# Low parts of the projections' weights made by ScalarE and an accumulating transfer in place of VectorE

## The chip, the core and the metric

The kernel runs on one core of one Trainium2 chip. Its time is the device time of one execution in microseconds (us); the median of several runs is what counts. One further execution was taken with the hardware profiler: its page and its trace are the source of every row below.

## What is computed

One inference step of a decoder layer, for 512 prompt tokens and 8 sampling tokens together (T = 520 columns). Cut to what matters here:

```python
hn = rms_norm(x, p['norm_mix'][l])
z = jnp.einsum('bld,de->ble', hn, p['w_in'][l])             # 2048 -> 4096
xa, ga, xb, gb, zc = jnp.split(z, [...], axis=-1)
# three token mixers side by side: RG-LRU (xa, ga), convolution (xb, gb), chunked gating (zc)
mix = jnp.concatenate([y_a, y_b, y_c], axis=-1)
x = x + jnp.einsum('blm,md->bld', mix, p['w_out'][l])       # 2048 -> 2048
hf = rms_norm(x, p['norm_ffn'][l])
ff = jnp.square(jax.nn.relu(jnp.einsum('bld,df->blf', hf, p['w_ff1'][l])))
x = x + jnp.einsum('blf,fd->bld', ff, p['w_ff2'][l])
y = rms_norm(x, p['norm_final'])
```

All of it is float32. A matrix product is made of three products of a shorter type, `fp32r`: each operand is split into a high part (the value rounded to fp32r) and a low part (the value less its high part, rounded likewise), and high x high, high x low and low x high are added up in PSUM.

## The kernel before

The two projections are cut into **units**. A unit is 1024 rows by 128 columns of a weight matrix, stored as a tile of 128 partitions x 1024 elements (512 KB), and holds eight 128x128 blocks. There are 96: units 0 to 63 are the input projection `w_in`, units 64 to 95 the output projection `w_out`. Then follow the two large products of the MLP, whose items are made by other code (`split_item`, `product`; lines 1071 to 1170) that the change does not touch.

Each unit passes through these steps. SyncE loads it into one of seven `raw` tiles (`load`, L149). ScalarE copies it, rounded, into a `whi` tile (`hi_part`, L154). VectorE writes raw less high into a `wlo` tile (`lo_part`, L160); after that the raw tile may be loaded again. TensorE then does 48 matmuls of 260 columns (`matmuls`): for each of the eight blocks two with high weights and high activations (L177), two with high weights and low activations (L179), two with low weights and high activations (L181). `whi` and `wlo` have four buffers each. A unit's high part can therefore be written once the matmuls of the unit four before it are done.

The order on every engine is written out by hand: an instruction runs in the order in which the program issues it on its engine, and waits there for what it needs. The main loop runs over units and MLP items, `i = 0` to `NU - 1`, and issues in this order: loads that may go (`more_weights`: up to five units ahead, and while more than one raw tile is free), the high part of unit `i + 3` (`AHEAD` is 3), the low part of unit `i + 3`, the matmuls of unit `i`, and, where a group of units is complete, its reading out of PSUM (`evac1`, L723 to L747). Last, `run(credit)` issues pieces of the mixers' work (L485 to L690: convolution, norms, gates, recurrence), by a budget of constants for each unit. Units 0 to 3 are split and multiplied in pieces as the activations arrive; units 4 to 7 are split ahead of the loop (low parts up to 7 are done there).

GpSimd does nothing large until the MLP. In the projections it only clears the heads of the padded tiles `xaf` and `ubf` (memsets, L700 and L713); from about 610 us it issues stores and loads of MLP operands (L905, L913, L1094). SyncE's queue also holds small loads and stores of the mixers (L489, L613, L690, L758), and issues in order, so loads of weights often go out several at a time behind one of these.

Of the kernel before, what the change touches and what calls it, by code (L numbers as in the profile page):

```python
# [6 lines left out]
F32R = mybir.dt.float32r  # L7
AF = mybir.ActivationFunctionType
ALU = mybir.AluOpType
# [57 lines left out]
def trunk_kernel(tc, xT, vecs, w_in, w_out, w_ff1, w2, ca_st, h0_st, cb_st, gate_w, sgu_wT, sgu_b,  # L67
                 yT, ca_o, lh_o, cb_o, cv_o):
    nc = tc.nc
    V, S, P, PE = nc.vector, nc.scalar, nc.gpsimd, nc.tensor  # L70
    from contextlib import ExitStack
    with ExitStack() as es:
# [5 lines left out]
        wp = es.enter_context(tc.tile_pool(name="wp", bufs=1))  # L78
# [8 lines left out]
        def nm(s):  # L87
            cnt[0] += 1
            return f"{s}_{cnt[0]}"
# [36 lines left out]
        raws, whis, wlos = {}, {}, {}  # L126
# [6 lines left out]
        def raw_drop(r):  # L133
            rfree.append(r[1])
# [16 lines left out]
        def hi_part(i, a=0, b=8):  # L151
            if i not in whis:
                whis[i] = wp.tile([128, 1024], F32R, tag="whi", name=nm("whi"), bufs=4)
            S.activation(out=whis[i][:, a * 128:b * 128], in_=raws[i][0][:, a * 128:b * 128], func=AF.Copy)  # L154

        def lo_part(i, a=0, b=8):
            if i not in wlos:
                wlos[i] = wp.tile([128, 1024], F32R, tag="wlo", name=nm("wlo"), bufs=4)
            sl = slice(a * 128, b * 128)
            V.tensor_tensor(out=wlos[i][:, sl], in0=raws[i][0][:, sl], in1=whis[i][:, sl].bitcast(F32),  # L160
                            op=ALU.subtract)
            if b == 8:
                raw_drop(raws.pop(i))
# [94 lines left out]
        def require(flag, name):  # L258

            if flag in flags:  # L260
                return
            while flag not in flags:
                if isinstance(advance(name), Wait):
                    for n in queues:
                        if n != name and queues[n]:
                            advance(n)
# [43 lines left out]
        units = []  # L310
# [15 lines left out]
        NP = len(units)  # L326
        LD, AHEAD = 4, 3
# [150 lines left out]
        sig, ubf, xaf, graw = {}, {}, {}, {}  # L478
# [214 lines left out]
        def evac1(kind, c, ps, mode=0):  # L693

            if kind == "xa":
                if mode < 2:
                    if c >= 2:
                        require(("conv_a", c - 2), "a")
                    xaf[c] = Tt(c % 2, 552)
                    P.memset(xaf[c][:, 0:3], 0.0)  # L700
                o = xaf[c][:, 3:3 + T].rearrange("p (h n) -> p h n", h=2)
            elif kind == "ga":
                if mode < 2:
                    mixt[c] = Mt(c)
                o = hv(mixt[c])
            elif kind == "gb":
                if mode < 2:
                    sig[c] = Zt()
                o = hv(sig[c])
            elif kind == "xb":  # L710
                if mode < 2:
                    ubf[c] = Tt(12 + c, 552)
                    P.memset(ubf[c][:, 0:30], 0.0)  # L713
                o = ubf[c][:, 30:30 + T].rearrange("p (h n) -> p h n", h=2)
            elif kind == "vc":
                mixt[12 + c] = Mt(12 + c)
                o = hv(mixt[12 + c])
            else:
                require(("head", 7), "a")
                gu[c] = Tt(5 + c)  # L720
                o = hv(gu[c])
            if mode == 1:
                S.activation(out=o, in_=pv(ps), func=AF.Copy)  # L723
                return
            V.tensor_tensor(out=o, in0=o if mode else pv(ps), in1=hv(R), op=ALU.mult)
            if kind == "xa":
                push("a", g_head(c))
                if c > 0:
                    require(("gates", c - 1), "a")
                    load_gate(c)  # L730
            elif kind == "ga":
                S.activation(out=mixt[c], in_=mixt[c], func=AF.Gelu_apprx_tanh)
            elif kind == "gb":
                S.activation(out=sig[c], in_=sig[c], func=AF.Sigmoid)
            elif kind == "xb":
                u = ubf[c][:, 30:30 + T]
                V.tensor_tensor(out=u, in0=u, in1=sig.pop(c), op=ALU.mult)
                push(f"b{c % 2}", g_conv_b(c))
                if c == 3:
                    push("n", g_norm_b())  # L740
            elif kind == "vc":
                S.activation(out=mixt[12 + c], in_=mixt[12 + c], func=AF.Gelu_apprx_tanh)
                if c == 3:
                    push("c", g_norm_c())
                    push("c", g_sgu())
            else:
                S.activation(out=gu[c], in_=gu[c], func=AF.Gelu_apprx_tanh)  # L747
                flags.add(("uc", c))
# [327 lines left out]
        for q in quads[32:]:  # L1076
            i, a, b = WIN[q.win]
# [153 lines left out]
        lo_done = 7  # L1231
        credit = 0.0
        for i in range(NU):
            it[0] = i
            if i > 3:
                more_weights()
            if 7 < i + AHEAD < NP:
                hi_part(i + AHEAD)
            while lo_done < min(i + AHEAD, NP - 1):
                lo_done += 1  # L1240
                lo_part(lo_done)
            run_due("v", i)
            if NP <= i + AHEAD < NU:
                split_item(i + AHEAD - NP)
            run_due("a", i)
            if i < NP:
                u = units[i]
                kind = u.grp[0]
                if i > 3:
                    matmuls(i, u)  # L1250
                if i == NP - 1:
                    for c in range(8, 16):
                        free.extend([(ap_, f"Ah{c}"), (ap_, f"Al{c}")])
            else:
                if i == NP:
                    psp.release()
                    ps2.append(es.enter_context(tc.tile_pool(name="ps2", bufs=1, space=bass.MemoryType.PSUM,
                                                             reuse_waits="tile")))
                product(i - NP)
                more_operands()  # L1260
                if i - NP == H1_DONE + 2:
                    fin = last_norm(1)
                if i - NP >= H1_DONE + 2:
                    next(fin, None)
            if i >= NP:
                continue
            if u.stop:
                ps = ps_of.pop(u.grp)
                if kind == "out":
                    kh, m = u.grp[1:]  # L1270
                    V.tensor_tensor(out=hv(x1[m]), in0=pv(ps), in1=hv(x1[m]), op=ALU.add)
                    if kh:
                        hf_half(m % 8, m // 8)
                elif i <= 6:
                    held.append(u.grp)
                    evac1(u.grp[0], u.grp[1], ps, 1)
                else:
                    evac1(kind, u.grp[1], ps)
            if i == 6:
                ps = bsum(ssum[0])  # L1280
                rstd(pv(ps), hv(R), hv(Zt()), 1.0 / D)
                V.tensor_scalar(Rp, R, 1.0, None, op0=ALU.min)
                for g in held:
                    evac1(g[0], g[1], None, 2)
            if i == 62:

                for c in range(8):
                    require(("y_a", c), "a")
                    mx[c] = At(c)
                    split_to(mx[c], mixt[c])  # L1290
                load_x1(0)
                load_x1(1)
            if i == 63:
                flags.add("hn")
            if kind == "out":
                kh, m = u.grp[1:]
                if kh == 0 and m + 2 < 16:
                    load_x1(m + 2)
                if kh == 0 and m == 15:
                    for c in range(8, 16):  # L1300
                        require(("mx", c), "c" if c >= 12 else "n")
                    drain()
                    mc.release()
                    xp = es.enter_context(tc.tile_pool(name="xp", bufs=1, reuse_waits="tile"))
                    free += [(mp, f"M{c}") for c in range(8, 16)] + [(tp, f"T{c}") for c in range(8, 16)]
                    free += [(xp, f"E{c}") for c in range(NX)]
                    for c in range(8):
                        free += [(ap_, f"Ah{c}"), (ap_, f"Al{c}")]
            if i < 80:
                credit = min(credit + UNIT_US - 1.2 - (1.0 if u.stop else 0.0), 6.0)  # L1310
                credit -= run(credit)
            else:
                run(0.7)
# [90 lines left out]
```

## Time and profile before

| | |
|---|---|
| median of 3 runs | 1910.35 us (1909.89 to 1910.84) |
| the profiled execution | 1910.32 us |
| its span (first to last instruction) | 1908.6 us |
| TensorE's mean granted clock | 0.994 |
| TensorE busy | 1874.4 us (98%) |
| VectorE busy | 1563.5 us (82%) |
| ScalarE busy | 968.5 us (51%) |
| GpSimd busy | 264.0 us (14%) |
| projections, matmuls of units 4 to 95 | 32.6 to 583.8 us |

The page gives the busy time of each engine and its share of the span; PE is TensorE (PEld its loads of weights), DVE VectorE, ACT ScalarE, POOL GpSimd, SP SyncE. In timelines the first two numbers are the start and the length in us, then come engine, line, operation and tiles (output<-inputs) and how many instructions one line merges. A bracket at the end gives the time that the engine stood idle before, and what ended it. "To landing" is the time from a transfer's issue to its arrival. Lines are those of the kernel before.

### The profile page before, as it was taken

The numbers are of one execution on the slowest core, as the hardware profiler recorded it, in microseconds if no ns is written. First come the engines' busy times: TensorE is split into PE (matmuls) and PEld (weight loads), VectorE is DVE, ScalarE is ACT, GpSimd is POOL, SyncE is SP. The second block draws the span as 40 slices with busy tenths as digits, with TensorE's granted clock in tenths as the row PEclk, the third lists the DMA queues.
The fourth block names the chain that finished last, engine by engine and source line by source line (L and its number), as shares of the span: only waits on it lengthen the run. The fifth ranks groups of instructions, "written<-read, shape, count | busy, mean of one in ns | idle before, by whom it ended". The sixth has DMA issues, their size and how long they took to land.

```text
span 1908.6 us, 38079 instructions
## 1 busy us (share of the span) xinstructions
PE 1874.4 (98%) x15540; PEld 1869.0 (98%) x15540; DVE 1563.5 (82%) x2206; ACT 968.5 (51%) x1443; POOL 264.0 (14%) x499
## 2 busy tenths in 40 slices
PE   8999999999999999999999999989999999999995
PEld 8999999999999999999999999989999999999994
DVE  7878777565688889899888888877798888888888
ACT  7445345562235666666666666644444444444453
POOL 0000000000000122122111121530312112112000
PEclk9999999999999999999999999999999999999997
DMA  6223223133343656656555555883757657647324
GB/s 253 106 95 117 72 95 114 59 139 113 122 167 124 217 200 218 216 201 220 202 184 209 194 197 206 302 319 103 277 162 241 228 197 236 204 153 262 116 85 134
DMA packets 113072, 336.82 MB, mean 176 GB/s; under 512 B 16768, under 2 KB 25600, under 8 KB 112896
## 3 DMA queue, kind: packets, MB, share of 16 engines
q1 hardware_dynamic: 73200, 205.35, 32.1%
q0 software_dynamic: 38400, 127.83, 18.9%
q8 instruction: 122, 2.00, 0.4%
q10 hardware_dynamic: 1296, 1.19, 0.2%
q14 instruction: 54, 0.44, 0.1%
HBM read 265.44 MB, written 68.87 MB: 175 GB/s over the span
## 4 chain that ended last, share of the span: by engine, by line
PE 95%; DVE 2%; DMA 1%; issue 1%; POOL 1%; ACT 0%; SPq 0%; DVEq 0%; POOLq 0%; ACTq 0%
PE psA L1167 12%; PE psA L1170 12%; PE psA L1169 12%; PE ps L181 10%; PE ps L179 10%; PE ps L177 10%; PE psD L1169 6%; PE psD L1167 6%; PE psD L1170 6%; PE psB L1170 3%; PE psB L1167 3%; PE psB L1169 3%; DVE X L1223 1%; DVE wlo L1147 0%; DMA raw<-w 0%
## 5 line engine op out<-in xcount | busy, mean ns | idle before, releaser
L1145 ACT ACTIVATE whi<-raw 128x1024 fp32r<-128x1024 f32 (+5 forms) x532 | 488.9, 921 | 327.5 <-PE psD L1169 143.1
L1147 DVE TENSOR_TENSOR wlo<-raw,whi 128x1024 fp32r<-128x1024 f32 (+5 forms) x532 | 558.8, 1051 | 88.2 <-ACT whi L1145 86.7
L1170 PE MATMUL psA<-o,wlo 128*128 128x260 f32 x2048 | 578.4, 282 | 2.8 <-DVE wlo L1147 2.8
L1167 PE MATMUL psA<-o,whi 128*128 128x260 f32 x2048 | 578.5, 282 | 1.9 <-DVE X L974 0.7
L1169 PE MATMUL psA<-o,whi 128*128 128x260 f32 x2048 | 577.8, 282 | 0.0
L1167 PEld LDWEIGHTS psA<-o,whi 128*128 128x128 f32 x2048 | 385.3, 188 | 3.2 <-DVE X L974 1.2
L1170 PEld LDWEIGHTS psA<-o,wlo 128*128 128x128 f32 x2048 | 385.2, 188 | 3.2 <-DVE wlo L1147 3.2
L1169 PEld LDWEIGHTS psA<-o,whi 128*128 128x128 f32 x2048 | 385.2, 188 | 0.0
L1101 DVE TENSOR_TENSOR raw<-raw,raw 128x1024 f32<-128x1024 f32 (+6 forms) x304 | 318.8, 1049 | 29.3 <-DMA raw<-w 28.9
L177 PE MATMUL ps<-Ah,whi 128*128 128x260 f32 x1536 | 311.5, 284 | 5.8 <-ACT Ah L356 5.8
L179 PE MATMUL ps<-Al,whi 128*128 128x260 f32 x1536 | 310.7, 284 | 0.0
L181 PE MATMUL ps<-Ah,wlo 128*128 128x260 f32 x1536 | 310.2, 283 | 0.0
L1170 PE MATMUL psD<-o,wlo 128*128 128x260 f32 x1024 | 289.3, 282 | 1.2 <-DVE wlo L1147 1.2
L1167 PE MATMUL psD<-o,whi 128*128 128x260 f32 x1024 | 289.8, 283 | 0.0
L1169 PE MATMUL psD<-o,whi 128*128 128x260 f32 x1024 | 289.7, 283 | 0.0
L177 PEld LDWEIGHTS ps<-Ah,whi 128*128 128x128 f32 x1536 | 238.4, 189 | 6.3 <-ACT Ah L356 6.1
L181 PEld LDWEIGHTS ps<-Ah,wlo 128*128 128x128 f32 x1536 | 238.2, 189 | 0.0
L179 PEld LDWEIGHTS ps<-Al,whi 128*128 128x128 f32 x1536 | 237.4, 190 | 0.6 <-DVE Al L359 0.6
L905 POOL DMA_DIRECT2D fx<-o x224 | 121.6, 543 | 815.3 <-DVE o L794 569.3
L1170 PEld LDWEIGHTS psD<-o,wlo 128*128 128x128 f32 x1024 | 192.8, 188 | 1.4 <-DVE wlo L1147 1.4
L1169 PEld LDWEIGHTS psD<-o,whi 128*128 128x128 f32 x1024 | 193.0, 188 | 0.0
L1167 PEld LDWEIGHTS psD<-o,whi 128*128 128x128 f32 x1024 | 192.7, 188 | 0.0
(207 smaller groups left out, 2282.7 us busy)
## 6 DMA issues: line engine op xcount, KB each, us to landing
raw<-w_ff SPq DMA_DIRECT2D x128, 512.0 KB, 4.1
fx<-o POOLq DMA_DIRECT2D x224, 260.0 KB, 3.1
o<-fx POOLq DMA_DIRECT2D x224, 260.0 KB, 5.0
raw<-w SPq DMA_DIRECT2D x116, 384.0 KB, 3.7
raw<-w_in SPq DMA_DIRECT2D x62, 512.0 KB, 6.0
raw<-w_out SPq DMA_DIRECT2D x32, 512.0 KB, 5.6
raw<-w SPq DMA_DIRECT2D x32, 448.0 KB, 3.5
z<-x1d POOLq DMA_DIRECT2D x32, 260.0 KB, 3.2
```

Of the source, the lines that this page charges most:

```text
L177: PE.matmul(ps[:, h, :H], hi[:, kk], xh[:, h * H:(h + 1) * H], start=st, stop=False)
L179: PE.matmul(ps[:, h, :H], hi[:, kk], xl[:, h * H:(h + 1) * H], start=False, stop=False)
L181: PE.matmul(ps[:, h, :H], lo[:, kk], xh[:, h * H:(h + 1) * H], start=False, stop=sp)
L905: P.dma_start(fxd[i][2 * g - 1 + n if g else 0], t[0][:, :].bitcast(F32))
L1101: V.tensor_tensor(out=o[0][:, :n], in0=x[0][:, :n], in1=y[0][:, :n], op=ALU.add)
L1145: S.activation(out=whis[i][:, :n], in_=r[0][:, :n], func=AF.Copy)
L1147: V.tensor_tensor(out=wlos[i][:, :n], in0=r[0][:, :n], in1=whis[i][:, :n].bitcast(F32), op=ALU.subtract)
L1167: PE.matmul(ps, hi[:, kk], xh, start=first and j == 0, stop=False, skip_group_check=True)
L1169: PE.matmul(ps, hi[:, kk], xl, start=False, stop=False, skip_group_check=True)
L1170: PE.matmul(ps, lo[:, kk], xh, start=False, stop=j == q.q - 1 and p in (("P2", "P3", "Q4", "P7") if q.late else ("P2", "P3", "Q4")), skip_ ...
L1223: V.scalar_tensor_tensor(out=x, in0=x, scalar=vc(V_FIN + m), in1=o, op0=ALU.mult, op1=ALU.mult)
```

## The change

For units 8 to 95 the low part is no longer made by VectorE. A new function, `both_parts`, takes the place of `hi_part` in the loop: ScalarE writes the high part as before, then a second time with scale -1, so that the low tile holds the negative of the high part. The raw tile is given up at once. GpSimd then issues a transfer that reads the unit's weights from memory once more, adds them to what stands in the low tile, and converts to fp32r: weights less high part, as before. Units 0 to 7 keep `lo_part`. The memsets of the padded tiles go from GpSimd to VectorE.

```diff
+        def both_parts(i):
+
+            hi_part(i)
+            wlos[i] = wp.tile([128, 1024], F32R, tag="wlo", name=nm("wlo"), bufs=4)
+            S.activation(out=wlos[i], in_=raws[i][0], func=AF.Copy, scale=-1.0)
+            raw_drop(raws.pop(i))
+            P.dma_start(wlos[i], units[i].src, accum_op=ALU.add)
...
-                    P.memset(xaf[c][:, 0:3], 0.0)
+                    V.memset(xaf[c][:, 0:3], 0.0)
...
-                    P.memset(ubf[c][:, 0:30], 0.0)
+                    V.memset(ubf[c][:, 0:30], 0.0)
...
             if 7 < i + AHEAD < NP:
-                hi_part(i + AHEAD)
-            while lo_done < min(i + AHEAD, NP - 1):
+                both_parts(i + AHEAD)
+            while lo_done < min(i + AHEAD, 7):
                 lo_done += 1
                 lo_part(lo_done)
```

## Rows read from the trace of the kernel before

**Rows 1.** The page: busy us (share of span) xinstructions, and the last chain's engines.

```profile
PE 1874.4 (98%) x15540; PEld 1869.0 (98%) x15540; DVE 1563.5 (82%) x2206; ACT 968.5 (51%) x1443; POOL 264.0 (14%) x499
...
PE 95%; DVE 2%; DMA 1%; issue 1%; POOL 1%; ACT 0%; SPq 0%; DVEq 0%; POOLq 0%; ACTq 0%
```

**Rows 2.** Windows: stretch, its us, busy of each engine; clock, DMA share, GB/s.

```profile
core 0: us, PE busy (x) PEld busy (x) DVE busy (x) ACT busy (x) POOL busy (x), PEclk, DMA share, GB/s
...
50.00:583.00 533.00, 533.00 (x4433) 532.40 (x4431) 388.16 (x575) 234.32 (x317) 0.72 (x8) 1.00 0.31 108
```

**Rows 3.** TensorE's waits: total us, times, longest; up to 700 us, then all.

```profile
PE ps L177 <- ACT Ah L356: 5.8, 2, 5.6
...
PE side L1202 <- DVE fsum L955: 6.7, 1, 6.7
...
PE psA L1170 <- DVE wlo L1147: 2.8, 2, 1.8
```

**Rows 4.** Lines L160 and L154: ns min/median/max, first and last start.

```profile
L160 DVE TENSOR_TENSOR wlo<-raw,whi x108: 415/1218/1228, 4.9 to 565.2; 128x1024 fp32r<-128x1024 f32 x92, 128x256 fp32r<-128x256 f32 x16
...
L154 ACT ACTIVATE whi<-raw x108: 398/1045/1065, 4.5 to 564.0; 128x1024 fp32r<-128x1024 f32 x92, 128x256 fp32r<-128x256 f32 x16
```

**Rows 5.** Line L1094, GpSimd's plain reads of 260 KB: issue ns, and landing us.

```profile
L1094 POOL DMA_DIRECT2D o<-fx x224: 546/546/563, 1196.5 to 1763.5; - x112
...
DMA to landing us min/median/max: 2.8/5.0/8.8
```

**Rows 6.** DMA view: issues of 316:328 and 60:63; the load queue of 389:406.

```profile
raw<-w_in SPq DMA_DIRECT2D x3, 512.0 KB, 3.6
...
raw<-w_in SPq DMA_DIRECT2D x5, 512.0 KB, 5.9
...
q1 hardware_dynamic: 1961, 5.36, 88.7%
```

**Rows 7.** Timeline of ScalarE, late in the projections: unit 93's high part.

```profile
552.46 1.04 ACT L154 ACTIVATE whi<-raw 128x1024 fp32r<-128x1024 f32 x1
```

**Rows 8.** Timeline of TensorE: first matmuls of units 10, 11, 61, 66, 93.

```profile
68.04 0.40 PE L177 MATMUL ps<-Ah,whi 128*128 128x260 f32 x2
...
68.52 0.28 PE L181 MATMUL ps<-Ah,wlo 128*128 128x260 f32 x1
...
73.80 0.40 PE L177 MATMUL ps<-Ah,whi 128*128 128x260 f32 x2
...
375.64 0.59 PE L177 MATMUL ps<-Ah,whi 128*128 128x260 f32 x2
...
404.62 0.41 PE L177 MATMUL ps<-Ah,whi 128*128 128x260 f32 x2
...
566.32 0.40 PE L177 MATMUL ps<-Ah,whi 128*128 128x260 f32 x2
```

**Rows 9.** Timeline of ScalarE: high parts of units 10, 11 and 12, 61 and 62, 66.

```profile
59.83 1.04 ACT L154 ACTIVATE whi<-raw 128x1024 fp32r<-128x1024 f32 x1
...
68.05 1.99 ACT L154 ACTIVATE whi<-raw 128x1024 fp32r<-128x1024 f32 x2
...
369.54 1.99 ACT L154 ACTIVATE whi<-raw 128x1024 fp32r<-128x1024 f32 x2
...
396.55 1.04 ACT L154 ACTIVATE whi<-raw 128x1024 fp32r<-128x1024 f32 x1
```

**Rows 10.** Timeline of VectorE: the subtraction of unit 10 and what follows.

```profile
65.65 1.22 DVE L160 TENSOR_TENSOR wlo<-raw,whi 128x1024 fp32r<-128x1024 f32 x1
66.78 0.69 DVE L725 TENSOR_TENSOR M<-ps,R 128x520 f32<-128x520 f32 x1
```

**Rows 11.** Timeline of SyncE's queue: two of the bursts of loads.

```profile
60.39 2.31 SPq L149 DMA_DIRECT2D raw<-w_in  x5
...
366.93 1.98 SPq L149 DMA_DIRECT2D raw<-w_out  x4
```

## The prediction

> **What bounds the kernel now.** I read the page first: its busy shares put TensorE at 98% of the span, VectorE at 82%, ScalarE at 51%, and in the chain of work that ended last 95% is TensorE and 2% VectorE [rows 1]. An average says little of one stage, so the table of windows came next, for the stretch that the change touches: units 8 to 95 of the projections. From 50 to 583 us TensorE is busy for all 533.00 us, at a granted clock of 1.00, while VectorE has 388 of them and the DMA engines 31% [rows 2]. Then the list of waits: in the first 700 us TensorE waited 5.8 us in all, twice, for the first activations (L356), before unit 8 is reached; its other waits (seven more lines of the list, the longest two 6.7 and 2.8 us) are in the second half or at the end, for L955, L1147 and their like, which the change leaves alone [rows 3]. So where VectorE is relieved, nobody waits for VectorE, and the stage lasts as long as its matmuls. What can still move the time is the other side: a low part that comes too late for its matmuls.
>
> **What goes.** 88 of the 108 subtractions L160 leave VectorE, those of units 8 to 95, 1.218 us each at the median [rows 4]: 88 x 1.218 = 107 us of VectorE's time. Worth on the path: 0, since TensorE waits for none of it [rows 2, 3]; VectorE's list of work after each unit is budgeted by constants in the code, and does not grow. Twelve small memsets come to VectorE from GpSimd, at some 0.1 us each, and are hidden in VectorE's idle 145 us of that stretch [rows 2].
>
> **What comes: ScalarE.** 88 activations that write the negative high part into the low tile. The nearest row is L154, the same tile and shape, at 1.045 us [rows 4]: 92 us, for an engine with some 234 of 533 us in use [rows 2]. Each stands directly behind L154 of its unit, so the low part starts its second leg about 1.04 us after the high part is done. Queued behind it on ScalarE are the gelu, sigmoid and square operations, which have the earlier VectorE in their favour: where ScalarE waits for VectorE, it now waits 1.2 us less per subtraction that stood in front.
>
> **What comes: GpSimd and the transfer.** 88 transfers of 512 KB, which read the weights in memory again and add them to the low tile. GpSimd has nothing else to do until its stores near 610 us. An issue costs it 0.546 us at the median [rows 5]. From the issue to the landing there is no row of an accumulating transfer, so I bound it. Lower end: a plain load of the same 512 KB on idle queues, 3.6 us [rows 6]. An accumulating one also has to read what stands in the tile. In the crowded stretch from 389 to 406 us the engines moved 5.36 MB at 88.7% busy, so 512 KB are 17 x 0.887 / 5.36 x 0.524 = 1.47 us of all 16 engines [rows 6]: one pass. With one more pass the transfer lands after 3.6 + 1.5 = 5.1 us when alone. It is seldom alone at the tight places: SyncE issues its loads in bursts of five, whose median landing is 5.9 us instead of 3.6 [rows 6]. Sharing the engines with such a burst costs between nothing and two passes more (3.0), so 5.1 to 8.1 us; I take the middle, 6.6 us, in a burst and 5.9 us at a burst's end. Upper end of all: four passes with a burst besides, some 12 us.
>
> The row that bears on the price is the pass of 1.47 us, and a second pass is my estimate from it [rows 6]. The Trainium skill, in "Collectives: The Full Stack" (section "The bandwidth ceiling: the fold count and why AG ≠ RS ≠ AR"), says that an add in the DMA path costs no cycles of its own, but two reads for each write, so half the rate of a copy; its "DMA: Bandwidth & Descriptors" (section "Anatomy of one DMA — SWDGE (gpsimd) path") gives 2.0 us + bytes / 436 GB/s, which for 1 MB read makes an estimate of 4.4 us. No row before shows such a transfer. By 4.4 us no unit below would be late, and the time would be that of before.
>
> **Where it is late.** In the usual case the high part is done at 553.5 us [rows 7] for a unit whose matmuls start at 566.3 [rows 8], 12.8 us later, and 11.8 us remain after the new activation: cover for any transfer up to that. I compared all 92 high parts with the start of their unit so; four units from 8 on have the least room (10, 11, 61, 66), the others 6.5 us or more after their added activation, once VectorE's earlier release is counted. A unit's low tile is first read 0.48 us after its first matmul (its two pairs with the high part come first) [rows 8].
> Unit 10: the high part runs from 59.83 to 60.87 us, the negative one to 61.91; with 6.6 us it lands at 68.5, in the burst that began at 60.39 [rows 9, 11]. It is needed at 68.04 + 0.48 = 68.52 [rows 8]: 0.0 us late.
> Unit 11: ScalarE starts its high part at 68.05, behind a gelu that waits for VectorE's L725 at 66.78, and this stands behind the subtraction of unit 10 (65.65) [rows 9, 10]. With that gone it starts 1.1 us earlier, near 66.95; both parts are done at 69.0; with 5.9 us it lands at 74.9. Needed at 73.80 + 0.48 = 74.28: 0.6 us late.
> Unit 61: two high parts stand together at 369.54 [rows 9]; the first and its negative are done at 371.6, in the burst that began at 366.93 [rows 11]. Landing at 378.2, needed at 375.64 + 0.48 = 376.12 [rows 8]: 2.1 us late. What holds ScalarE up there hangs on matmuls of its own (L660), so this adds to the 0.6.
> Unit 66: its high part starts at 396.55 [rows 9], at the end of ten microseconds in which ScalarE has no gap (L295, L553), so unit 65's added activation moves it to 397.6, and both parts are done at 399.7. In the crowd of loads 6.6 to 8.1 us: 406.3 to 407.8. Needed at 404.62 + 0.48 = 405.1, and at 407.8 after the 2.7 us already lost [rows 8]: 0.
> **Sum**: 0.0 + 0.6 + 2.1 + 0 = 2.7 us lost, nothing won. On the profiled execution's 1910.3 us (span 1908.6 us, 1.7 us around it; the median is 1910.35, the same within 0.1) that is 1913.0 us. What is lost is not regained: from 50 us to the second half TensorE has no idle time to give.
>
> **The rivals.** A: the transfer is slower by some passes, 9 us or a little more from issue to landing. Then unit 10 is 61.9 + 9 - 68.5 = 2.4 us late, unit 11 69.0 + 9 - 74.3 = 3.7 (the first included), unit 61 adds 4.5, and with 10.5 us in the bursts 6 + 6 and a few us at units with 9 us of room: 8 to 15 us, 1918 to 1925. It decides from about 7.7 us in a burst, where the sum passes 3.8 us. For it: GpSimd's crowded plain reads of only 260 KB need 5.0 us at the median and 8.8 at most [rows 5]. Against: those stand in a stage with far more traffic.
> B: the transfer is bound by rate. A unit lasts about 5.75 us (68.04 to 73.80) [rows 8]; a plain load takes 1.47 of it, so an add of more than some 2.9 passes (4.3 us of all engines) fills the DMA engines and sets the pace. At four passes 88 x (7.35 - 5.75) = 141 us are lost, 2051 us. It is the one case in which all 88 units pay.
> C: the relief wins something. The whole projections hold only the 5.8 us of waiting, all ahead of unit 8 [rows 3]; for a gain the second half would have to run better for the shift, and the longest wait there is 6.7 us [rows 3].
> D: no lateness at all, the transfer at its lower end: 1910.3, in the same class as the forecast.
>
> **How the numbers follow.** About 0.2%, 3.8 us, is what a measurement of this kernel can tell from no change. Forecast with D, 0 to 3.8 us: 0.51. A: 0.33. B: 0.13. C: 0.03. The likeliest is the forecast, 1913.0. The range takes in the unchanged time and all of A and leaves B out: 1909.5 to 1925.
>
> **What would show it.** After the change: VectorE's L160 with 20 entries, ScalarE busier by some 92 us, q0 with 46 MB more; TensorE's waits between 50 and 583 us for the low tile, released by the transfer, two or three of them, at units 10, 11 and 61 and about 3 us together; the transfers' median landing near 5 to 6 us. I am wrong if that median is over 8 us, if such waits stand at units with 12 us of cover, or if the DMA share in the projections rises from 0.31 to near 0.9 instead of some 0.6 to 0.8.

## The result and the profile after

The changed kernel takes 1923.49 us at the median (1922.64 to 1924.10, 4 runs), the kernel before 1910.59 beside it: a ratio of 1.0069, 95% interval 1.0056 to 1.0081. It is slower by 12.9 us, which is rival A's side of the range, not the likeliest case of 1913.0.

The page of the changed kernel (first the busy time of the engines, then the shares of the chain that ended last; before: [rows 1]):

```profile
PE 1879.3 (98%) x15540; PEld 1873.1 (98%) x15540; DVE 1463.1 (76%) x2130; ACT 1052.4 (55%) x1531; POOL 336.6 (18%) x575
...
PE 90%; issue 4%; DMA 3%; DVE 2%; POOL 0%; ACT 0%; DVEq 0%; SPq 0%; POOLq 0%; ACTq 0%
```

VectorE lost 100 us of work and ScalarE got 84, as meant. TensorE's share is still 98%: the number that a reader looks at first does not show the loss. The chain does: 3% DMA where there was 1%. The windows show the stage (the columns are those of [rows 2], which this row answers):

```profile
50.00:583.00 533.00, 524.80 (x4332) 523.37 (x4331) 279.66 (x484) 311.22 (x396) 73.90 (x86) 0.99 0.77 190
```

TensorE stood idle for 8.2 us of a stretch that was full before, it did 4332 matmuls in it instead of 4433, the granted clock is 0.99, and the DMA share went from 0.31 to 0.77. The list of waits says for whom (total us, times, longest; before: [rows 3]):

```profile
PE ps L189 <- DMA wlo<-w_in: 8.1, 3, 4.2
```

L189 is the product with the low weights (L181 before). Its places, in TensorE's timeline (units 10, 51 and 61; the bracket is the idle time before the line):

```profile
66.65 0.40 PE L187 MATMUL ps<-Al,whi 128*128 128x260 f32 x2
71.27 0.68 PE L189 MATMUL ps<-Ah,wlo 128*128 128x260 f32 x2 [4.21 <-DMA wlo<-w_in]
...
320.68 0.50 PE L189 MATMUL ps<-Ah,wlo 128*128 128x260 f32 x2 [1.25 <-DMA wlo<-w_in]
...
385.21 0.61 PE L189 MATMUL ps<-Ah,wlo 128*128 128x260 f32 x2 [2.64 <-DMA wlo<-w_in]
```

Three waits of 8.1 us do not make 12.9. The rest is in the clock. Windows around the first and the last of these waits (same columns; the number behind the busy times is the granted clock):

```profile
66.00:71.20 5.20, 1.05 (x9) 0.84 (x7) 4.99 (x10) 5.20 (x7) 1.73 (x2) 1.00 1.04 283
71.20:74.60 3.40, 3.33 (x16) 3.34 (x17) 3.37 (x9) 0.23 (x2) 0.85 (x1) 0.53 1.07 213
74.60:78.00 3.40, 3.40 (x29) 3.40 (x29) 2.16 (x5) 0.77 (x3) 0.00 (x0) 0.96 1.04 211
...
385.20:388.60 3.40, 3.38 (x16) 3.39 (x17) 2.47 (x4) 3.37 (x5) 0.27 (x1) 0.54 0.96 188
```

Behind the wait of unit 10, and behind that of unit 61, TensorE ran for 3.4 us at the lower of its two clock levels (1.2 GHz): 16 matmuls in such a window, where 31 fit at full clock (shown below). That is 1.6 to 1.8 us each. Behind the 1.25 us of unit 51 nothing of the kind follows.

Where each unit's 48 matmuls take longer, from first start to last end, than in the trace before:

| unit | longer by, us | of it waiting for the transfer | transfer's issue to landing, us |
|---|---|---|---|
| 10 | 6.0 | 4.4 | 10.7 |
| 27 and 39 together | 0.2 | under 0.1 | 9.1, 9.4 |
| 51 | 1.5 | 1.4 | 10.4 |
| 61 | 4.4 | 2.8 | 7.1 |
| 66 | 0.4 | 0.3 | 8.4 |
| sum | 12.5 | 8.9 | |

The third column is how much later than before the first low product starts, counted from the unit's first matmul, so it holds a little more than the brackets. Of the other 3.6 us, 1.6 each at units 10 and 61 are the clock. The sum is what the projections grew by (units 4 to 95 last 563.7 us, 551.1 before), and it agrees with the 12.9 us of the medians. The spans (1920.9 and 1908.6) differ by 12.3, because this execution's projections began 1.6 us earlier (unit 4 at 31.0 instead of 32.6 us) and what follows them took 1.4 us more, with one more 3.4 us of half clock near 1263 us, in a part that the change does not touch.

### The profile page after: what moved, and what is told of

It reads as the page before. It is cut to its first block, busy times and chain, and to the rows that moved or that the text cites. A ratio compares the mean times of both kernels' runs of the same rounds, so it can differ in the third digit from the quotient of the medians.

```text
span 1920.9 us, 38226 instructions
## 1 busy us (share of the span) xinstructions
PE 1879.3 (98%) x15540; PEld 1873.1 (98%) x15540; DVE 1463.1 (76%) x2130; ACT 1052.4 (55%) x1531; POOL 336.6 (18%) x575
## 4 chain that ended last, share of the span: by engine, by line
PE 90%; issue 4%; DMA 3%; DVE 2%; POOL 0%; ACT 0%; DVEq 0%; SPq 0%; POOLq 0%; ACTq 0%
PE psA L1175 12%; PE psA L1178 12%; PE psA L1177 12%; PE ps L189 8%; PE ps L185 8%; PE ps L187 8%; PE psD L1175 6%; PE psD L1177 6%; PE psD L1178 6%; PE psB L1178 3%; PE psB L1175 3%; PE psB L1177 3%; DMA wlo<-w_in 1%; DVE X L1231 1%; DVE wlo L1155 1%
## 5 line engine op out<-in xcount | busy, mean ns | idle before, releaser
L189 PE MATMUL ps<-Ah,wlo 128*128 128x260 f32 x1536 | 311.5, 284 | 8.2 <-DMA wlo<-w_in 8.1
L189 PEld LDWEIGHTS ps<-Ah,wlo 128*128 128x128 f32 x1536 | 238.8, 190 | 9.2 <-DMA wlo<-w_in 8.7
```

Source lines behind the costliest of these rows:

```text
L189: PE.matmul(ps[:, h, :H], lo[:, kk], xh[:, h * H:(h + 1) * H], start=False, stop=sp)
```

## The experiments

The theory after the result: all of the loss is TensorE waiting for transfers that land late at a few units, and the low clock behind the two long waits; landing is late where a transfer meets a burst of SyncE's loads. The rivals: S, ScalarE's 88 added activations delay things by themselves; T, the added traffic slows everything a little; Q, the burst alone is the price, and the add is not. Each was timed beside the kernel before (1909.9 to 1910.4 us at the median there).

**No transfer.** The low tile keeps the negative high part.

```diff
-            P.dma_start(wlos[i], units[i].src, accum_op=ALU.add)
```

> The changed kernel without its 88 accumulating transfers; ScalarE still writes the negative high parts, and the low parts of units 8 to 95 are left out of the result. Theory (all the loss is TensorE waiting for the transfers at a few units, and a lower clock after the two long waits): 1910.6 us, ratio 1.000 to the kernel before, no wait of TensorE between 50 and 590 us. Rival S (ScalarE's 88 added activations hold things up): still 1915 to 1923 us.

Measured: 1910.30 us, ratio 1.0000 (0.9991 to 1.0009). Windows:

```profile
50.00:583.00 533.00, 533.00 (x4435) 532.52 (x4434) 292.05 (x502) 314.98 (x402) 0.00 (x0) 1.00 0.31 108
```

ScalarE has all of its added work (315 us, in place of 234 in [rows 2]), and TensorE no idle time. Rival S falls: the whole loss hangs on the transfer.

**Ten units given back to VectorE.**

```diff
+ON_DVE = (10, 11, 27, 39, 51, 52, 61, 62, 66, 67)
...
-                both_parts(i + AHEAD)
-            while lo_done < min(i + AHEAD, 7):
-                lo_done += 1
-                lo_part(lo_done)
+                if i + AHEAD in ON_DVE:
+                    hi_part(i + AHEAD)
+                    lo_part(i + AHEAD)
+                else:
+                    both_parts(i + AHEAD)
```

> The changed kernel with ten units (10, 11, 27, 39, 51, 52, 61, 62, 66, 67) made by VectorE as before; 78 transfers stay. Theory: 1911 us, at most 2 us over before, no wait over 1 us in the projections, no stretch of half clock. Rival T (the added traffic slows everything a little): 78/88 of the 12.9 us stay, 1922 us.

Measured: 1910.07 us, ratio 1.0000 (0.9992 to 1.0009). Windows:

```profile
50.00:583.00 533.00, 533.00 (x4435) 532.52 (x4434) 302.00 (x510) 306.24 (x393) 65.24 (x76) 1.00 0.73 184
```

The DMA share is 0.73, nearly that of the changed kernel, and nothing is lost. Rival T falls: 78 transfers that land in time cost nothing.

**Low products last.** The 32 matmuls with the high weights first, then the 16 with the low ones.

```diff
             for k in range(a, b):
...
-                    PE.matmul(ps[:, h, :H], lo[:, kk], xh[:, h * H:(h + 1) * H], start=False, stop=sp)
+            for k in range(a, b):
+                xh, xl = u.xs(k)
+                kk = slice(k * 128, k * 128 + 128)
+                for h in (0, 1):
+                    PE.matmul(ps[:, h, :H], lo[:, kk], xh[:, h * H:(h + 1) * H], start=False,
+                              stop=u.stop and k == 7)
```

> The changed kernel with each unit's 48 matmuls in another order: all 32 with the high weights first, then the 16 with the low ones, so that the low tile is needed 3.84 instead of 0.48 us after the unit's start. Theory: the waits of 4.4, 3.0 and 1.4 us at units 10, 61 and 51 shrink by 3.36 each, to 1.0, 0 and 0, and no half clock: 1911.6 us. Rival T (traffic): about 1922 us still.

Measured: 1911.85 us, ratio 1.0008 (0.9999 to 1.0016). Windows:

```profile
50.00:583.00 533.00, 533.00 (x4423) 532.41 (x4423) 288.01 (x497) 315.26 (x402) 73.97 (x86) 1.00 0.77 193
```

All 88 transfers are there and land as late as before (10.2 us for unit 51, 9.5 for unit 10); with 3.36 us more of cover TensorE stands idle for none of them. So it is lateness against the moment of need, and nothing else about the transfers, that costs. Most of what is left (1.5 us at the median) belongs to the new order itself: with no wait anywhere each unit lasts 0.01 us longer, and units 4 to 95 together 552.3 us, 1.1 more than before.

**Matmuls in the waits.** Extra matmuls, of no use, into the columns of the PSUM tile that nobody reads, ahead of the first low product.

```diff
+FILL = {10: 34, 61: 24}
...
+                for n in range(FILL.get(i, 0) if k == 0 else 0):
+                    PE.matmul(ps[:, n % 2, H:512], hi[:, kk], xh[:, :512 - H], start=False, stop=False)
```

> The changed kernel with 34 extra matmuls (into unused PSUM columns) ahead of the first low matmul of unit 10 and 24 at unit 61, some 4.0 and 2.8 us of TensorE work in place of the waits of 4.4 and 3.0. Theory with the clock: no stretch of half clock follows, 1.6 us are saved at each, 1920.3 us. Without the clock's part (the loss would be the waits alone): 1923.5 us, unchanged.

Measured: 1920.19 us (1919.54 to 1921.17), ratio 1.0056 (1.0043 to 1.0068). Each against the kernel before beside it, that is 9.8 us over, 3.1 less than the changed kernel's 12.9; no run of the one reaches a run of the other. The same windows as shown above:

```profile
66.00:71.20 5.20, 5.20 (x47) 5.20 (x46) 5.02 (x8) 4.51 (x6) 0.88 (x1) 1.00 1.04 300
71.20:74.60 3.40, 3.40 (x31) 3.40 (x30) 3.29 (x9) 2.13 (x3) 1.70 (x2) 1.00 1.09 276
...
385.20:388.60 3.40, 3.40 (x30) 3.40 (x30) 3.30 (x5) 3.13 (x3) 0.87 (x1) 1.00 0.73 145
```

The clock stays at 1.00, here and in all of the projections, and 31 and 30 matmuls fit where 16 did. TensorE waits just as long for the data, only busily, and the kernel gains about the two times 1.6 us that were expected (units 4 to 95 last 560.6 us instead of 563.7). So waits of 4.2 and 2.6 us cost 1.6 us more each in the clock.

**A plain transfer.** The low tile then holds the weights themselves.

```diff
-            P.dma_start(wlos[i], units[i].src, accum_op=ALU.add)
+            P.dma_start(wlos[i], units[i].src)
```

> The changed kernel with its 88 transfers plain (read and convert, no add), so that the low tile holds the weights themselves and the result is not the reference's. Theory (an add is two passes of the DMA engines, a plain transfer one): landing alone falls from 5.5 to about 4.0 us, the DMA share of 50:583 from 0.77 to about 0.54, the waits at units 10, 61 and 51 to 1 us or less each, no half clock: 1912 to 1914 us. Rival Q (the place in the queue behind a burst of loads is the price, not the add): landing at unit 10 still over 9 us, 1919 us or more.

Measured: 1913.64 us (1910.67 to 1915.77), ratio 1.0020 (1.0011 to 1.0030). Line L162 (issue to landing), the DMA view of 50:583 (packets, MB, share of 16 engines), and the waits:

```profile
DMA to landing us min/median/max: 3.7/4.6/8.9
...
q0 software_dynamic: 12384, 45.09, 27.2%
...
PE ps L189 <- DMA wlo<-w_in: 3.3, 2, 2.1
```

The same two rows of the changed kernel:

```profile
DMA to landing us min/median/max: 5.3/6.7/12.4
...
q0 software_dynamic: 12454, 45.32, 47.7%
```

For the same bytes written the add keeps the engines busy 47.7 / 27.2 = 1.75 times as long, and lands 1.6 us later when alone (5.3 and 3.7). The total fell into the expected range; the single waits did not: 2.1 and 1.3 us at units 10 and 61, not 1 or less, since even the plain transfer of unit 10 took 8.6 us. The add is only part of what was late there. No half clock followed these waits, as expected.

**Half of each tile.** The transfer makes columns 0 to 511, VectorE the others.

```diff
-            S.activation(out=wlos[i], in_=raws[i][0], func=AF.Copy, scale=-1.0)
+            S.activation(out=wlos[i][:, 0:512], in_=raws[i][0][:, 0:512], func=AF.Copy, scale=-1.0)
+            V.tensor_tensor(out=wlos[i][:, 512:1024], in0=raws[i][0][:, 512:1024],
+                            in1=whis[i][:, 512:1024].bitcast(F32), op=ALU.subtract)
...
-            P.dma_start(wlos[i], units[i].src, accum_op=ALU.add)
+            P.dma_start(wlos[i][:, 0:512], units[i].src[:, 0:512], accum_op=ALU.add)
```

> The changed kernel with the accumulating transfer for the first 512 of each unit's 1024 columns and VectorE's subtraction for the other 512. Theory: half the passes, so DMA share near 0.54, landing alone near 4 us, waits together under 2 us: 1910.5 to 1912.5 us. If the price of a transfer were fixed and not its passes: about 1920 us.

Measured: 1915.08 us (1912.41 to 1917.74), ratio 1.0026 (1.0017 to 1.0035): more than was expected. Line L164 and the waits:

```profile
DMA to landing us min/median/max: 3.6/4.5/10.0
...
PE ps L191 <- DMA wlo<-w_in: 3.5, 2, 2.0
```

The median landing is shorter, as expected, but unit 10's transfer of half the bytes still took 9.0 us and held TensorE for 2.0 (again with no half clock behind it). The run changes more than the bytes: GpSimd now issues a transfer only after VectorE's half is written as well, and 47 of the 88 issues waited for that. Unit 10's did not suffer by it (issued at 60.10 us, in the changed kernel at 60.47). This execution (1912.41 us) is the quickest of its kernel, so the others must have lost more; how their loss is spread is not known. With the plain transfer it says that rival Q is largely right about unit 10.

**Nothing ahead of the loads.** The four stores of `cb_o` and those of `ca_o` and `lh_o` go from SyncE to ScalarE.

```diff
-            nc.sync.dma_start(cb_o[:, c], cbs[:, 0:270])
+            S.dma_start(cb_o[:, c], cbs[:, 0:270])
...
-                nc.sync.dma_start(ca_o, cao)
-                nc.sync.dma_start(lh_o, lho)
+                S.dma_start(ca_o, cao)
+                S.dma_start(lh_o, lho)
```

> The changed kernel with the six stores of mixer states that SyncE's loads queue behind (four of cb_o, ca_o, lh_o) issued by ScalarE instead, so that the loads ahead of units 10 and 61 no longer come in bursts of five. Rival Q and the theory both say that landing at unit 10 falls from 10.7 to 5.5 to 7 us and its wait from 4.4 to under 1; unit 61 keeps 1 to 2 us; unit 51's burst stands behind another transfer (gate_w) and stays with 1.4 us. Sum 3 to 5 us, no half clock: 1913.5 to 1915.5 us. If bursts are not the cause, 1923 us.

Measured: 1915.13 us (1914.18 to 1917.48), ratio 1.0027 (1.0017 to 1.0037). The changed kernel around unit 10, ScalarE, SyncE's queue and GpSimd:

```profile
59.14 1.04 ACT L160 ACTIVATE wlo<-raw 128x1024 fp32r<-128x1024 f32 x1
...
58.31 0.35 SPq L497 DMA_DIRECT2D cb_o<-T  x1
58.75 2.61 SPq L149 DMA_DIRECT2D raw<-w_in  x5
...
60.47 0.84 POOL L162 DMA_DIRECT2D wlo<-w_in  x1 [13.81 <-ACT wlo L160]
```

The store (58.31) waits for ScalarE, five loads wait behind it and leave together, and 1.7 us after the first of them the transfer of unit 10 joins. In the experiment the only loads of that time leave from 41.30 us, as raw tiles come free, and unit 10 lands after 5.4 us instead of 10.7:

```profile
41.30 5.63 SPq L149 DMA_DIRECT2D raw<-w_in  x3
...
PE ps L189 <- DMA wlo<-w_in: 4.7, 5, 1.3
```

Unit 10 no longer waits, unit 61 lands after 5.5 us and waits 1.1, no window is at half clock. But units 27, 39 and 51, where the bursts stand behind a load of gate weights (L621), take 10.3 to 10.5 us and hold TensorE for about 1.1 us each.

**No bursts at all.** These loads go to ScalarE too.

```diff
-            nc.sync.dma_start(graw[c], gate_w[:, c])
+            S.dma_start(graw[c], gate_w[:, c])
```

> As the run with the six stores on ScalarE, and the small loads of gate weights (L621) issued by ScalarE too, so that nothing but weights stands in SyncE's queue in the first 370 us and loads go out one by one. Theory with bursts as the cause of late landings: units 27, 39 and 51 land after 5.5 to 7 us instead of 10.3 to 10.5 and no longer wait; unit 61 keeps its 1.0 us, unit 66 about 0.5: 1911.5 to 1913 us. If another cause makes them late: 1915 us, as in that run.

Measured: 1917.21 us (1916.05 to 1918.50), ratio 1.0040 (1.0027 to 1.0052): no quicker than the run before it (1.0027, and the intervals overlap), a miss. Unit 51 does land earlier (7.0 us) and does not wait, but 27 and 39 still take 9.1 us, and units 10 and 11 wait again (1.1 and 1.6). SyncE's queue and GpSimd at unit 27, and line L162:

```profile
162.99 0.33 SPq L149 DMA_DIRECT2D raw<-w_in  x1
...
163.37 0.87 POOL L162 DMA_DIRECT2D wlo<-w_in  x1 [10.60 <-ACT wlo L160]
...
DMA to landing us min/median/max: 5.3/7.8/11.3
```

A load waits for a raw tile, and the raw tile comes free when ScalarE has read it the second time; the transfer waits for the same activation. With nothing else in SyncE's way the two leave together, unit after unit. From the landings of both lines up to 385 us, the median time of a transfer by the number of weight loads in flight with it:

```
loads in flight      0     1     2     3     4     5     6     8
changed kernel     5.5   6.0   7.2   8.1   9.1   8.7   9.4  11.4   (18, 8, 2, 5, 7, 5, 9, 2 transfers)
no bursts          6.1   7.8   7.9   8.1  10.0                     (4, 6, 21, 25, 1 transfers)
```

With the bursts 26 of 56 transfers meet at most one load, without them 10 of 57. So bursts are what makes the worst landings, but a queue of single loads is no remedy: it puts a load beside nearly every transfer.

**Both remedies.**

> Both remedies together on the changed kernel: no bursts, and each unit's low products last. Theory: no wait of TensorE in the projections, and then nothing more to win, since before had none either: 1910 us, the same as the kernel before. A time clearly below before would mean that relieving VectorE is worth something after all.

The edits of the last run and of the reordered products together. Measured: 1912.42 us (1910.76 to 1914.04), ratio 1.0014 (1.0005 to 1.0023). That is 2.5 us over, a little more than was expected. One wait of 1.0 us (unit 11) is left in the projections, and the order of the products costs its 1.1 us here too:

```profile
PE ps L190 <- DMA wlo<-w_in: 1.0, 1, 1.0
```

Nothing falls below the kernel before. No kernel of the study beats it; the best that keeps transfers only equals it.

## Why the prediction was right or wrong

**That the relief of VectorE is worth nothing: right.** VectorE's busy time in the stage fell from 388 to 280 us, and with the lateness taken away (ten units given back) the time is that of before. ScalarE's added work costs nothing either, as put: 88 activations of 1.04 us, the 92 us that were estimated (the busy time rose by 84, since an activation directly behind another overlaps it by 0.09 us), and a ratio of 1.0000 without the transfer.

**That lateness at a few units decides: right, with the units nearly right.** 10, 61 and 66 were named and were late; 11 was not, because unit 10's loss had moved its need by 6 us (with unit 10 in time, in the run with the six stores on ScalarE, unit 11 waited 0.3 us); 51 was missed. I had ranked the units by room alone. Unit 51 has 9 us of it, but it meets the longest burst (eight loads behind L621). One reading was off: unit 61's first low product stood at 376.31 us in the trace before, 0.67 and not 0.48 us behind its first matmul, so its lateness was 1.9 by the forecast's own terms and not 2.1. Nor is rival A's first 6 its own sum, which gives 69.0 + 10.5 - 74.3 = 5.2. Neither changes a choice.

**The transfer alone: right.** 5.1 us were worked out, 5.3 at the least and 5.5 with no load in flight were measured. Two passes were supposed; the share of the engines says 1.75 times a plain one, and the DMA share rose to 0.77, within the 0.6 to 0.8 that was put down. The median landing of all 88 was 6.7 us, above the 5 to 6 that were expected and below the 8 that would have been a sign of error. GpSimd's issue takes 0.857 us, not the 0.546 of [rows 5]:

```profile
L162 POOL DMA_DIRECT2D wlo<-w_in x56: 838/857/1030, 43.4 to 382.4; - x56
```

The estimate of 4.4 us that I worked out from the Trainium skill ("DMA: Bandwidth & Descriptors", section "Anatomy of one DMA — SWDGE (gpsimd) path") is 0.9 us below the quickest of 88. The other rule of the Trainium skill, two reads for each write ("Collectives: The Full Stack", section "The bandwidth ceiling: the fold count and why AG ≠ RS ≠ AR"), which the page states of a ring's ReduceScatter, is near the 1.75.

**The transfer in a burst: the step that failed.** I took 6.6 us, the middle between 5.1 and 8.1. Measured: 10.7, 10.4, 8.4 and 7.1 us at units 10, 51, 66 and 61. The upper bound of 8.1 rested on two passes of other work at most, a cost of 3.0 us over the transfer alone; unit 10's transfer took 5.2 us more than one alone. The DMA views of the changed kernel show where they went (packets, MB, share of 16 engines; q1 is the loads' queue, q0 the transfers'). Unit 10's transfer was issued at 60.47 us. First the view from 60.5 to 65.1 us, which has no row of q0, then that from 65.1 to 69.5:

```profile
q1 hardware_dynamic: 386, 1.41, 93.4%
...
q0 software_dynamic: 140, 0.52, 60.5%
q1 hardware_dynamic: 194, 0.72, 43.5%
```

The view of 92 to 98 us has a transfer with no load beside it, issued at 92.10 us (the first line is the engines' busy share in 40 slices of 0.15 us):

```profile
DMA  0000000000099092949949696959696811000000
...
q0 software_dynamic: 144, 0.52, 56.0%
```

Alone, the first packet moves 1.56 us after the issue and the last of the 144 has landed 4.0 us later. In the burst the first moved only 4.64 us after the issue, while the loads had the engines, and 6.1 us more went by to the landing: 3.1 us lost before the start and 2.1 behind it. The bound had a price for sharing the engines and none for a late start. The start was as late without the add and with half of the bytes: the same view of the plain transfers from 60.1 to 64.2 us, and of the half transfers from 60.1 to 64.6, with unit 10's issued at 60.14 and 60.10, has no row of q0 either:

```profile
q1 hardware_dynamic: 371, 1.39, 93.9%
...
q1 hardware_dynamic: 391, 1.45, 92.6%
```

With the burst out of the way (the six stores on ScalarE), unit 10's first packet moved 1.6 us after its issue. So the burst makes the late start; the add lengthens what follows it (6.1 us from the first packet to the landing at unit 10, 4.5 in the plain run). With 10.7 in place of 6.6 the sum's first term is 61.9 + 10.7 - 68.5 = 4.1 us, which is the wait that was found; at unit 61, with 7.1 us, the forecast 2.1 us became 2.6.

**The clock: a term that was missing.** I priced a wait of TensorE at its own length. The two longest cost 1.6 us more each at half clock; filling them with matmuls gave 3.1 us back. This (3.2 us) and the waits (8.9 us; 2.7 were forecast) are 12.1 of the projections' 12.5 us; the other 0.4 is spread over units 27, 39, 51 and 66, where the first pair of products behind a late tile runs longer (0.50 us at unit 51, 0.41 as a rule).

**The chances.** The likeliest case was put at no change, 0.51, on a margin of about 1 us in a term whose bounds were 3 us apart and one of them wrong. Rival A named the mechanism, the units and 1918 to 1925 us, and is what happened, except that its "slower by some passes" was in the main a later start beside a burst and not more passes. The range held because it took in A. That A's figure came so near is in part luck: 3.2 of the 12.9 us are the clock, for which it had no term. Rival B did not come: units with 11.8 us of cover never waited.

## What to carry to other kernels

An engine that is 80% busy is no reason to relieve it: where TensorE has no wait in a stage, the most that a change there can do is to add one. A longer route for an operand is priced at the worst landing at the tightest unit, beside the largest burst that can be in flight, and not at its median (here 10.7 us against 6.7); and a stall of several microseconds on TensorE is priced with the low clock behind it. Where the operand must come late, its use is put late: moving the low products to the end of each unit took the loss from 12.9 us to 1.5, which the interval (0.9999 to 1.0016) does not tell from none.

## What was not expected of the hardware

A transfer that GpSimd issued beside a burst of plain loads did not start at once: in the changed kernel the first packet moved 4.1 to 4.6 us after the issue at units 10, 27, 39 and 51, and 1.5 to 1.7 us after it where no load and no other transfer was in flight. Leaving out the add, or half of the bytes, hardly changed that (4.1 and 4.5 us at unit 10). Why the start waits is open; it does not wait for the whole burst, since three of the five loads landed 2.9 to 8.5 us after unit 10's transfer had begun. TensorE's granted clock fell to about half for 3.4 us behind idle times of 4.21 and 2.64 us; no such window stood behind the 1.25 us of unit 51, nor behind the 2.1 us of the plain transfer's unit 10.
